# The RWKV-7 chunk scan of a hybrid encoder, rewritten from block-diagonal 128x128 matmuls to matmuls on 64x64 tiles of the array

## The chip, the cores and the metric

The kernel runs on one core of a Trainium2 chip. The metric is the device time of one execution in microseconds (us); lower is better. Engines are named as in the profile: PE is the matmul engine and PEld its weight loads, DVE the vector engine, ACT the scalar engine, POOL the GpSimd, SP the queue that issues most DMAs.

## The reference

Two layers on 256 + 1024 = 1280 tokens of width 1024 (16 heads of 64). Layer 0 mixes tokens with a bidirectional RWKV-7 recurrence, layer 1 with neighbourhood attention; a squared-ReLU MLP follows each. The change lies in the recurrence of layer 0, which is this, for each head and both directions:

```
def _wkv_scan(r, w, k, v, a, b, reverse):
    def step(S, inp):
        r_t, w_t, k_t, v_t, a_t, b_t = inp
        sa = jnp.einsum('bhvk,bhk->bhv', S, a_t)
        S = S * w_t[:, :, None, :] + sa[..., None] * b_t[:, :, None, :] + v_t[..., None] * k_t[:, :, None, :]
        return S, jnp.einsum('bhvk,bhk->bhv', S, r_t)
...
    mu = jnp.mean(y, axis=-1, keepdims=True)
    var = jnp.mean(jnp.square(y - mu), axis=-1, keepdims=True)
    y = ((y - mu) * lax.rsqrt(var + GN_EPS)).reshape(B, T, C) * lnx_g + lnx_b
    y = y + (bonus * vf).reshape(B, T, C)
    out = (y.astype(h.dtype) * g) @ w_o
```

## The kernel before

The recurrence is computed in chunks of 64 tokens. For a chunk, products of the decayed vectors a, r with b, k give 64x64 matrices; the one of a and b is unit-triangular and is inverted; then the chunk needs only matmuls with the 64x64 state S of a head.

**Jobs and units.** The work is cut into ten *jobs* (`self.jobs`, L721): two of the short sequence, eight of the long one. A job has 16 chunks of a pair of heads (two heads of 64 lie in the 128 partitions) and runs them forwards (d = 0) and backwards (d = 1). A *unit* is one step of both directions, so the scan has 160 units.

**Order.** Nothing is scheduled by the compiler: every piece is a closure with a due time in units, put on a list by `at(time, ...)`, sorted, and recorded in that order (`manual_schedule`); each engine takes its instructions in that order. Job j is due from 16 j on. Pieces whose last argument is level 1 or 2 (job 0's early work) run already during the v projection, before `scan()`.

**The chain of a unit** (`scan_step`, once for each direction, half a unit apart): `s0` multiplies k-products with v into `w` (L1012); `s1` adds ar.S (L1023) and copies the two diagonal 64x64 blocks to `up` (L1027); `s2` multiplies with the inverse (L1032), copies to `hv` (L1034) and, in `s2c`, the two blocks to `u` (L1041); `s3` makes the new state (L1046), which DVE scales block by block (L1054) and adds to the decayed old one that POOL made (`sd`, L1016); `s4` adds the rest of the output (L1060), which ACT or DVE puts into `y` (L1063, L1065). Each of these is one 128x128 matmul on a block-diagonal operand: half of each such operand is zeros.

**The work beside the chain**, done for groups of four chunks, eight groups a job, one every two units: `prod` (a.b products, L812, masked by DVE, L814), `kprod` (k products, L953, copied by ACT, masked by POOL, L958), `ktr` (transposes, L967, copied by ACT, L970), and the inverse. Its 32x32 halves are inverted on DVE for a whole job at once: 31 rank-1 steps (`rank1`), two DVE instructions each (L857, L859), laid over ten units; the halves are joined by 32x32 matmuls (`merge1` L903, `merge2` L921). Operands come by DMA, some of them twice, because the block-diagonal copies (`bb`, `bdk`, `vt`) are loaded apart.

**After the chain** `scan_post` normalises each half of a job's outputs on DVE (L1116 to L1163), ACT (square) and POOL (gain and bias), transposes it on PE (L1168) and stores it. `gate_begin` puts loads and splits for the next stage beside the last job. PSUM: three rotating buffers (`aps`) for the work beside the chain, five banks for the chain.

Of the kernel before, what the change touches and what calls it, by code (L numbers as in the profile page):

```python
# [23 lines left out]
NEG = -1e30  # L24
L2_EPS = 1e-24
# [3 lines left out]
V_QG, V_KG = 136, 137  # L29
NVEC = 138  # L30
# [18 lines left out]
class Trunk:  # L49
    def __init__(self, ctx, tc, a):  # L50
# [16 lines left out]
        self.dall = self.cp.tile([P, 8, 2, 20], F32, name="dall")  # L67
        self.bonus = self.cp.tile([P, 10, NH], F32, name="bonus")
# [33 lines left out]
    def l0_proj(self):  # L102
# [10 lines left out]
        W = 1283  # L113

# [400 lines left out]
    def prep_open(self, bctx):  # L515
        nc, tc, a = self.nc, self.tc, self.a
        self.ar_d = self.dram("ar_d", [8, 2, P, 20, P])
        self.bk_d = self.dram("bk_d", [8, 2, P, 20, P])
# [117 lines left out]
    def prep_products(self, U, h, i):  # L636
# [7 lines left out]
        if "ar" not in u:  # L644
            for nm in ("ar", "bk"):
                u[nm] = pk.tile([P, 8, P], F32, name=nm, tag=nm)
            u["kd"] = pk.tile([P, 512], F32, name="kd", tag=f"kd{d}", bufs=2)
            u["st"] = [(self.ar_d[m, d, :, ch0:ch0 + nch, :], u["ar"][:, :nch, :]), (self.bk_d[m, d, :, ch0:ch0 + nch, :], u["bk"][:, :nch, :])]
        ar, bk, kd = u["ar"], u["bk"], u["kd"][:, :w]
        if i == 0:  # L650
            nc.vector.tensor_tensor(out=ar[:, :nch, 64:128], in0=c3(r), in1=ec[:, :nch, 1 - d:65 - d], op=ALU.mult)
# [4 lines left out]
        elif i == 3:  # L656
            nc.vector.tensor_tensor(out=bk[:, :nch, 64:128], in0=c3(kd), in1=emc, op=ALU.mult)
        elif i == 4:
            nc.vector.scalar_tensor_tensor(out=tha, in0=tha, scalar=1.0, in1=kk, op0=ALU.add, op1=ALU.mult)
        elif i == 5:  # L660
            nc.vector.scalar_tensor_tensor(out=ar[:, :nch, 0:64], in0=c3(kk), scalar=-1.0, in1=ec[:, :nch, d:64 + d], op0=ALU.mult, op1=ALU.mult)
        elif i == 6:
            nc.vector.scalar_tensor_tensor(out=bk[:, :nch, 0:64], in0=c3(tha), scalar=0.5, in1=emc, op0=ALU.mult, op1=ALU.mult)
# [25 lines left out]
    def prep_bonus(self, U, h, step):  # L689
# [6 lines left out]
        elif step == 1:  # L696
            u["pb"] = self.ppn.tile([P, 8], F32, name="bps", tag="bps")
            for b in range(nb):
                nc.tensor.matmul(u["pb"][:, 2 * b:2 * b + 2], u["kd"][:, b * P:(b + 1) * P], self.blk, start=True, stop=True)
        else:  # L700
            nc.vector.tensor_copy(self.bonus[:, c0 // P:c0 // P + nb, 2 * m:2 * m + 2], u["pb"][:, :2 * nb].rearrange("p (b h) -> p b h", h=2))
# [6 lines left out]
    def scan_begin(self):  # L708
# [8 lines left out]
        self.r_hv, self.r_v2, self.r_q = ([[er.tile(shape, F32, name=name + "0")], 0] for name, shape in  # L717
                                          (("hv", [P, 16, P]), ("v2", [P, 16, P]), ("qq", [P, 16, 2, 64])))
        self.r_bb, self.r_ar, self.r_zb = ([[er.tile([P, 4, P], F32, name=f"{name}{i}") for i in range(n)], 0] for name, n in
                                           (("bb", 3), ("ar", 10), ("zb", 10)))  # L720
        for t in self.r_bb[0]:  # L721
            nc.gpsimd.memset(t, 0.0)
# [17 lines left out]
    def scan(self):  # L740
        nc, tc, pool = self.nc, self.tc, self.spool
        rp = self.rp = pool("rp", 1)
        fx = pool("fx", 1)

        def grow(r, pl, name, shape, n=1):
            r[0] += [pl.tile(shape, F32, name=f"{name}{len(r[0]) + i}") for i in range(n)]
        grow(self.r_hv, fx, "hv", [P, 16, P])
        grow(self.r_v2, fx, "v2", [P, 16, P])
        grow(self.r_q, fx, "qq", [P, 16, 2, 64])
        grow(self.r_ar, rp, "ar", [P, 4, P], 10)  # L750
        grow(self.r_zb, rp, "zb", [P, 4, P], 10)
        self.r_bk, self.r_u2, self.r_u1, self.r_s = [[], 0], [[], 0], [[], 0], [[], 0]
        grow(self.r_bk, fx, "bdk", [P, 4, P], 2)
        self.sp = pool("sp", 4)
# [3 lines left out]
        self.pbank = [self.pw.tile([P, 2, P], F32, name=f"us{d}") for d in range(2)]  # L758
        for r, nm, n in ((self.r_u2, "u2", 4), (self.r_u1, "u1", 3), (self.r_s, "S", 4)):
            grow(r, fx, nm, [P, P], n)  # L760
        for r in (self.r_bk, self.r_v2, self.r_u2, self.r_u1, self.r_s, self.r_q):
            for t in r[0]:
                nc.gpsimd.memset(t, 0.0)
# [13 lines left out]
    def scan_job(self, j):  # L777
# [4 lines left out]
        J = {"ar": {}, "zb": {}, "zk": {}, "lt": {}}  # L782
        order = [(0, 0), (1, 3), (0, 1), (1, 2), (0, 2), (1, 1), (0, 3), (1, 0)]


        T0 = -34.0

        def first(J=J):
            J["dd"] = [self.dsc.tile([16, 2, 64, 64], F32, name="dd", tag="dd") for _ in range(2)]
        at(T0, first, min(j + 1, 3))  # L790
        for n, (d, g) in enumerate(order):
            m, c0 = grp[g]
            t = T0 + 2 * n
            E = 1 if j == 0 else 2 if j == 1 and n < 2 else 3

            def load(d=d, g=g, m=m, c0=c0):
                ar = self.nxt(self.r_ar)
                nc.sync.dma_start(ar, self.ar_d[m, d, :, c0:c0 + 4, :])
                bb = self.nxt(self.r_bb)
                for e in range(2):  # L800
                    es = slice(64 * e, 64 * e + 64)
                    nc.sync.dma_start(bb[es, :, es], self.bk_d[m, d, es, c0:c0 + 4, 0:64])
                J["ar"][d, g], J["bb", d, g] = ar, bb

            def prod(c, d=d, g=g):
                ar, bb = J["ar"][d, g], J["bb", d, g]
                if c == 0:
# [1153 lines left out]
```

## Time and profile before

| what | value |
|---|---|
| median of 3 runs | 4312.45 us (4303.99 to 4316.88) |
| the profiled execution: its own time, its span | 4314.01 us, 4312.1 us |
| first and last `s0` matmul of the scan (L1012) | 763.7 and 1561.9 us |
| busy over the span | PE 3991.1, PEld 3342.6, DVE 2660.7, ACT 1813.1, POOL 1426.1 us |
| granted TensorE clock, mean | 0.958 |

The page has the span in 40 slices of 107.8 us; the scan lies in slices 8 to 15. A matmul of fp32 operands appears in the profile as two records (640 for the 320 matmuls of L1012), each with its own weight load; a record lasts from its start to the end of its pipeline, so that records in a row overlap, and the distance of their starts, not their length, is what they cost PE.

### The profile page before, as it was taken

Reading aid. Unit: us, or ns where it says so; the run is one execution under the profiler, and the core shown is the slowest. Engines: PE = TensorE matmul, PEld = TensorE weight load, DVE = VectorE, ACT = ScalarE, POOL = GpSimd, SP = SyncE. Lnnn points to the kernel's source line nnn. Section 1 sums busy time; section 2 is a strip of 40 time slices with the busy share of each in tenths; the row PEclk is TensorE's granted clock in tenths of the full one; section 3 lists DMA queues with packets and bytes.
Section 4 is the critical chain, followed back from the end, with each engine's and each line's share of the span. In section 5 each row is a group of like instructions: output and inputs, shape, how many; then the busy total and the mean of one; then the engine's idle time right before and its main releaser. Section 6 shows DMA issues by size and latency. Waiting matters only on the chain.

```text
span 4312.1 us, 69598 instructions
## 1 busy us (share of the span) xinstructions
PE 3991.1 (93%) x25060; PEld 3342.6 (78%) x25060; DVE 2660.7 (62%) x5390; ACT 1813.1 (42%) x4803; POOL 1426.1 (33%) x1498
## 2 busy tenths in 40 slices
PE   7888878888998879999999998999998999999999
PEld 4665668777777758888888888877676888888888
DVE  7889963577787654755555555166665655555555
ACT  6766641677777753111111123355554311111111
POOL 5440001234444443422222234144444432222222
PEclk9997879899999989999999999999998999999999
DMA  3335565566666434111111104333335211111111
GB/s 120 81 107 198 196 201 144 141 157 155 153 151 153 108 97 133 38 39 36 40 35 40 40 31 152 117 72 77 78 70 161 65 40 40 40 35 39 35 40 59
DMA packets 484537, 400.25 MB, mean 93 GB/s; under 512 B 289216, under 2 KB 392864, under 8 KB 484192
## 3 DMA queue, kind: packets, MB, share of 16 engines
q1 hardware_dynamic: 447968, 328.56, 28.1%
q10 hardware_dynamic: 34416, 61.35, 3.9%
q0 software_dynamic: 1808, 5.90, 0.4%
q8 instruction: 197, 3.23, 0.3%
q14 instruction: 148, 1.21, 0.1%
HBM read 285.66 MB, written 121.24 MB: 94 GB/s over the span
## 4 chain that ended last, share of the span: by engine, by line
PE 69%; DVE 14%; ACT 6%; DMA 5%; issue 4%; POOL 2%; SPq 1%; ACTq 0%; DVEq 0%; POOLq 0%
PE ps L97 17%; PE ps L99 16%; PE ps L98 16%; PE w L1060 2%; PE us L1032 2%; PE kps L953 1%; PE aps L812 1%; PE vps L503 1%; PE vps L505 1%; PE vps L504 1%; PE op L1876 1%; PE us L1046 1%; PE w L1012 1%; DVE S L1054 1%; ACT u L1041 1%
## 5 line engine op out<-in xcount | busy, mean ns | idle before, releaser
L1433 DVE TENSOR_TENSOR x<-ps,x 128x256 f32<-128x256 f32 x1488 | 814.1, 595 | 628.3 <-PE ps L99 628.0
L97 PE MATMUL ps<-ah,whi 128*128 128x512 f32 (+1 forms) x2304 | 843.1, 366 | 5.0 <-ACT whi L91 4.2
L99 PE MATMUL ps<-ah,wlo 128*128 128x512 f32 (+1 forms) x2304 | 824.0, 358 | 2.1 <-POOL wlo L92 2.0
L98 PE MATMUL ps<-al,whi 128*128 128x512 f32 (+1 forms) x2304 | 823.5, 357 | 2.6 <-POOL al L1323 2.6
L92 POOL TENSOR_TENSOR wlo<-raw,whi 128x1024 fp32r<-128x1024 f32 (+1 forms) x178 | 390.5, 2194 | 851.9 <-ACT whi L91 807.8
L97 PE MATMUL ps<-hh,whi 128*128 128x512 f32 (+1 forms) x1536 | 546.9, 356 | 13.8 <-DVE x L1433 13.8
L99 PE MATMUL ps<-hh,wlo 128*128 128x512 f32 (+1 forms) x1536 | 545.9, 355 | 0.0
L98 PE MATMUL ps<-hl,whi 128*128 128x512 f32 (+1 forms) x1536 | 545.2, 355 | 0.0
L97 PEld LDWEIGHTS ps<-ah,whi 128*128 128x128 f32 x2304 | 438.8, 190 | 80.2 <-issue 13.1
L91 ACT CAST whi<-raw 128x1024 fp32r<-128x1024 f32 (+1 forms) x206 | 200.7, 975 | 696.5 <-PE ps L98 630.6
L99 PEld LDWEIGHTS ps<-ah,wlo 128*128 128x128 f32 x2304 | 437.8, 190 | 67.8 <-POOL wlo L92 2.9
L98 PEld LDWEIGHTS ps<-al,whi 128*128 128x128 f32 x2304 | 438.5, 190 | 63.0 <-POOL al L1323 2.9
L1412 POOL TENSOR_TENSOR rl<-rl 128x512 f32<-128x512 f32 (+1 forms) x192 | 174.3, 908 | 500.6 <-PE ps L99 458.3
L97 PEld LDWEIGHTS ps<-hh,whi 128*128 128x128 f32 x1536 | 291.4, 190 | 57.4 <-DVE x L1433 16.8
L1411 ACT ACTIVATE rl<-ps 128x512 f32<-128x512 f32 (+1 forms) x192 | 100.8, 525 | 546.4 <-PE ps L99 546.4
L98 PEld LDWEIGHTS ps<-hl,whi 128*128 128x128 f32 x1536 | 291.4, 190 | 41.0
L99 PEld LDWEIGHTS ps<-hh,wlo 128*128 128x128 f32 x1536 | 291.4, 190 | 41.1
L1414 ACT CAST hh<-rl 128x512 fp32r<-128x512 f32 (+1 forms) x192 | 105.5, 549 | 321.0 <-POOL rl L1412 320.9
L1054 DVE SCALAR_TENSOR_TENSOR S<-us,dall,sd 64x64 f32<-64x64 f32 x512 | 145.0, 283 | 126.4 <-PE us L1046 115.7
L1415 DVE TENSOR_TENSOR hl<-rl,hh 128x512 fp32r<-128x512 f32 (+1 forms) x192 | 119.4, 622 | 151.6 <-ACT hh L1414 151.1
L1016 POOL TENSOR_TENSOR sd<-S,dall 128x128 f32<-128x128 f32 x256 | 122.5, 480 | 258.2 <-DVE S L1054 174.8
L1060 PE MATMUL w<-u,zb 128*128 128x128 f32 x640 | 158.2, 330 | 47.0 <-ACT u L1041 44.8
(310 smaller groups left out, 8222.4 us busy)
## 6 DMA issues: line engine op xcount, KB each, us to landing
raw<-in_w_down_dram SPq DMA_DIRECT2D x64, 512.0 KB, 3.5
raw<-in_w_up_dram SPq DMA_DIRECT2D x64, 512.0 KB, 3.4
ar<-ar_d SPq DMA_DIRECT2D x80, 256.0 KB, 3.4
bk<-bk_d SPq DMA_DIRECT2D x80, 256.0 KB, 3.5
ar_d<-ar ACTq DMA_DIRECT2D x32, 512.0 KB, 2.7
bk_d<-bk ACTq DMA_DIRECT2D x32, 512.0 KB
bs<-tab SPq DMA_DIRECT2D x128, 96.0 KB, 3.9
v_d<-vt ACTq DMA_DIRECT2D x80, 128.0 KB, 4.0
```

What stands on the lines that cost most here:

```text
L91: nc.scalar.copy(hi[:, cs], raw)
L92: lo_eng.tensor_tensor(out=lo[:, cs], in0=raw, in1=hi[:, cs].bitcast(F32), op=ALU.subtract)
L97: mm(ps, sh, mh, start=first, stop=False)
L98: mm(ps, sh, ml, start=False, stop=False)
L99: mm(ps, sl, mh, start=False, stop=last)
L1016: nc.gpsimd.tensor_tensor(out=R["sd"], in0=st["S"], in1=self.dall[:, m, d, ch:ch + 1].to_broadcast([P, P]), op=ALU.mult)
L1054: nc.vector.scalar_tensor_tensor(out=S2[es, es], in0=sn[es, es], scalar=D, in1=R["sd"][es, es], op0=ALU.mult, op1=ALU.add)
L1060: nc.tensor.matmul(w, J["zb"][d, g][:, c, :], R["u2"], start=False, stop=True, skip_group_check=True)
L1412: nc.gpsimd.tensor_tensor(out=r[:, :n], in0=r[:, :n], in1=r[:, :n], op=ALU.mult)
L1414: nc.scalar.copy(hh[:, :n], r[:, :n])
L1415: nc.vector.tensor_tensor(out=hl[:, :n], in0=r[:, :n], in1=hh[:, :n].bitcast(F32), op=ALU.subtract)
L1433: nc.vector.tensor_tensor(out=xv, in0=ps[:, :n], in1=xv, op=ALU.add)
```

## The change

- All scan matmuls become 64x64: operands of head 0 lie in partitions 0 to 63, of head 1 in 64 to 127, and `HALVES` runs over both. A matmul takes the row strip of its operands and the column strip of its output, so (0,0), (0,64), (64,0), (64,64) are four tiles. Block-diagonal copies and their DMAs go.
- One step treats both directions: `s1` adds a.S, r.S and (through the identity) S itself into three PSUM banks; ACT copies 128x128 (`s1c`, `s2c`) and writes the new state with two scaled copies (`s3c`). DVE and POOL no longer touch S.
- `kprod` masks straight from PSUM on DVE, `ktr` yields two transposes, all of them in the same three `aps` buffers. `merge1`/`merge2` become 64x64 matmuls on a zero-filled inverse, which POOL clears for each job (`qclear`).
- `rank1`: the threshold that closes a slot of half a unit goes from 877.08 to 930.0, and the start from T1 + 2.77 to T1 + 1.9.
- `scan_post`: the output stays in halves by head; gain and bias are applied after the transpose by one ACT instruction for each run; bonus times v is transposed apart; POOL has no part. `prep_bonus`, `ar_d`/`bk_d`, `dall`, `bonus` change layout; `gate_begin` changes due times.

The core of the diff (`-` before, `+` after):

```diff
-            load += 400 + 2 * jj * (32 - jj)
-            if load > 877.08:
+            if load > 930.0:
...
+            def prod(h, d=d, g=g):
+                    for c in (2 * h, 2 * h + 1):
+                        for es, eo in HALVES:
+                            mm(J["pa"][es, c], J["bb", d, g][es, c], J["aa", d, g][es, c], start=True, stop=True)
...
+                        for es, eo in HALVES:
+                            mm(J["pb"][es, c], bb[es, c], rr[es, c], start=True, stop=True)
+                            mm(J["pk"][eo, c, 0:64], kk[es, c], aa[es, c], start=True, stop=True)
+                        for es, eo in HALVES:
+                            mm(J["pk"][eo, c, 64:128], kk[es, c], rr[es, c], start=True, stop=True)
+                    nc.vector.tensor_tensor(out=zk, in0=J["pk"], in1=b4(self.mask[d], P), op=ALU.mult)
+                    nc.vector.tensor_tensor(out=zr, in0=J["pb"], in1=b4(self.mask[d][:, 64:128], 64), op=ALU.mult)
...
-            nc.tensor.matmul(R["w"], J["zk"][d, g][:, c, :], J["vt"][:, cc, :], start=True, stop=new)
+                for es, eo in HALVES:
+                    mm(A[es, d], zk[eo, c, 0:64], v[eo, cc], d == 0, new)
+                    mm(Y[eo, yd], zk[eo, c, 64:128], v[eo, cc], d == 0, False)
+                    for es, eo in HALVES:
+                        mm(sn[es, d], J["lk", d, g][eo, c], v[eo, cc], d == 0, False)
...
-                nc.tensor.matmul(w, J["ar"][d, g][:, c, :], S, start=False, stop=True)
+                for es, eo in HALVES:
+                    mm(A[es, d], J["aa", d, g][es, c], S[es, d], False, True)
+                    mm(Y[eo, yd], J["rr", d, g][es, c], S[es, d], False, False)
+                        mm(sn[es, d], self.ident[es, es], S[es, d], False, False)
+            nc.scalar.copy(R["up"], A)
...
-            nc.tensor.matmul(us, J["Q"][:, cc].rearrange("p d t -> p (d t)"), R["up"], start=True, stop=True)
+                    mm(U[es, d], J["Q"][es, cc, d], R["up"][es, d], True, True)
+            nc.scalar.copy(R["u"], U)
...
-                    nc.vector.scalar_tensor_tensor(out=S2[es, es], in0=sn[es, es], scalar=D, in1=R["sd"][es, es], op0=ALU.mult, op1=ALU.add)
+                        mm(sn[es, d], J["lb", d, g][es, c], R["u"][es, d], False, True)
+                    mm(Y[eo, yd], J["zr", d, g][es, c], R["u"][es, d], False, True)
+                nc.scalar.activation(S[:, d], sn[:, d], AF.Copy, scale=self.dall[:, m, d, ch:ch + 1])
...
+            def tr(src, nm, st=st):
+                for b in range(8):
+                    for es, eo in HALVES:
+                        nc.tensor.matmul(ps[es, b], src()[eo, b // 4, b % 4], self.ident[eo, eo], start=True, stop=True)
```

How the order of instructions moves, at three places (a row is a line of the source, the operation, out<-in, and the shape; rows of the change have the line numbers of the changed file, where L993 is the helper through which the chain's matmuls go).

PE, before, in the middle of a job: one direction's half of a unit, from its `s4` to the next one's `s4`.

```order
L1060 MATMUL w<-u_7184,zb_7159 128x128
L1012 MATMUL w<-v_6174,zk 128x128
L1032 MATMUL us_7181<-u_7188,qq_6175 128x128
L1023 MATMUL w<-S_7191,ar_7149 128x128
L812 MATMUL aps<-ar_6187,bb_6178 128x128 x2
L1046 MATMUL us_7180<-hv_6173,lt 128x128
L812 MATMUL aps<-ar_6187,bb_6178 128x128 x2
L1060 MATMUL w<-u_7185,zb_7160 128x128
```

PE, after: the end of `s1` of a unit, then `prod` of a group, `s2`, and half of the next unit's `s0` (`ba` is the bank A, `by` Y, `bs` the state's bank, `vv` is v, `cst` holds the identity).

```order
L993 MATMUL ba<-S,aa_7398 64x64
L993 MATMUL by_7443<-S,rr 64x64
L993 MATMUL bs_7445<-S,cst 64x64 x4
L812 MATMUL aps<-aa_6427,bb_6436 64x64 x8
L993 MATMUL by_7442<-up,qq_6417 64x64 x4
L993 MATMUL ba<-vv_6416,zk 64x64
L993 MATMUL by_7442<-vv_6416,zk 64x64
L993 MATMUL ba<-vv_6416,zk 64x64
L993 MATMUL by_7442<-vv_6416,zk 64x64
L993 MATMUL bs_7444<-vv_6416,lk 64x64 x2
```

Eight matmuls of 128 columns stood in half a unit; now a whole unit has 36 of 64 columns in the chain, and eight stand between `s1` and `s2` where two waits of the chain lie.

DVE, before, while a job's inverse is made: rank-1 pairs (`tmp`, `q`) between the state's updates (`S`) of the two directions.

```order
L857 TENSOR_TENSOR tmp<-mt,q 128x252
L859 TENSOR_TENSOR q<-q,tmp 128x14x18
L1054 SCALAR_TENSOR_TENSOR S_7189<-us_7181,dall,sd 64x64 x2
L857 TENSOR_TENSOR tmp<-mt,q 128x247
L859 TENSOR_TENSOR q<-q,tmp 128x13x19
L1054 SCALAR_TENSOR_TENSOR S_7190<-us_7180,dall,sd 64x64 x2
L814 TENSOR_TENSOR zb_6189<-aps,cst 128x512
```

DVE, after, in the same stretch: the pairs stand beside the masks that free PSUM (`zk`, `zr`, `za`) and the norm's first half (`bv`, `mu`).

```order
L858 TENSOR_TENSOR tmp<-mt,q 128x220
L860 TENSOR_TENSOR q<-q,tmp 128x22x10
L948 TENSOR_TENSOR zk<-kps,cst 128x512
L951 TENSOR_TENSOR zr<-bps,cst 128x256
L858 TENSOR_TENSOR tmp<-mt,q 128x231
L860 TENSOR_TENSOR q<-q,tmp 128x21x11
L858 TENSOR_TENSOR tmp<-mt,q 128x240
L860 TENSOR_TENSOR q<-q,tmp 128x20x12
L1097 TENSOR_TENSOR bv<-vv_7391,bonus 128x512
L815 TENSOR_TENSOR za_6440<-aps,cst 128x256
L1101 TENSOR_REDUCE mu<-y 128x8
L1102 TENSOR_SCALAR mu<-mu 128x8
```

The state's updates have left DVE; the masks and the norm have come closer to the rank-1 pairs, of which four now fall in each unit.

ACT, after, one unit: the chain's three copies, the state's two scaled copies among them, with a copy beside the chain (`yt`).

```order
L1034 COPY up<-ba 128x128
L908 COPY yt<-yps 128x256
L1045 COPY u<-by_7443 128x128
L1060 ACTIVATE S<-bs_7444,dall 128x64 x2
L1066 COPY y<-by_7442 128x2x64
```

Before, ACT had five copies of 64x64 or 64x128 for each direction's half unit, and the state was DVE's.

More of the change, by code (lines that the diff above doesn't have):

```diff
@@ L113, in l0_proj @@
         W = 1283
+        kp = self.sctx.enter_context(tc.tile_pool(name="kp", bufs=1))
+        self.dall = kp.tile([P, 8, 2, 20], F32, name="dall")
+        self.bonus = kp.tile([P, 12, 20], F32, name="bonus")
         mixctx = ExitStack()
@@ L816, in store @@
[L816 to L824 removed]
+                J["aa", d, g], J["bb", d, g] = self.nxt(self.r_aa), self.nxt(self.r_bb)
@@ L1066, in scan_step @@
[L1066 to L1071 removed]
+                nc.vector.tensor_tensor(out=y, in0=Y, in1=y, op=ALU.add)
+        at(i - 0.64, s0)
+        at(i, s1)
+        at(i + 0.1, s1c)
+        at(i + 0.3, s2)
+        at(i + 0.38, s2c)
+        at(i + 0.58, s3)
         if not end:
[L1073 to L1074 removed]
+            at(i + 0.66, s3c)
+        at(i + 0.75, s4)
```

495 lines of the change are left out of this document (218 added, 277 removed).

## The prediction

> **What bounds the kernel now.** First I asked where the scan stands and how busy each engine is in it. Busy time by stretches, a job in the middle, the last job, the stretch ahead of the scan (columns: length, busy time and instructions of each engine, granted clock, DMA share, GB/s):
>
> ```profile
> core 0: us, PE busy (x) PEld busy (x) DVE busy (x) ACT busy (x) POOL busy (x), PEclk, DMA share, GB/s
> 1003.00:1082.00 79.00, 70.41 (x733) 61.37 (x732) 62.34 (x168) 58.27 (x230) 37.52 (x65) 1.00 0.66 157
> 1480.00:1562.00 82.00, 66.40 (x605) 55.81 (x605) 39.32 (x113) 59.89 (x233) 36.46 (x56) 0.95 0.28 83
> 700.00:763.00 63.00, 48.80 (x379) 46.90 (x378) 24.64 (x60) 7.72 (x20) 11.95 (x25) 0.83 0.53 134
> ```
>
> A job takes some 80 us, a unit 5.0, and the last job as long, though DVE has only 39 us to do there: DVE does not set the pace now. The line of the first matmul of each step says how long the scan is:
>
> ```profile
> L1012 PE MATMUL w<-v,zk x640: 275/275/421, 763.7 to 1561.9; 128*128 128x128 f32 x160
> ```
>
> From first to last start are 798 us. Next, what PE pays. Groups of instructions in one job (x count | busy us, mean ns | idle before), and two stretches of the timeline:
>
> ```profile
> L1060 PE MATMUL w<-u,zb 128*128 128x128 f32 x64 | 15.6, 326 | 3.0 <-ACT u L1041 2.9
> L1046 PE MATMUL us<-hv,lt 128*128 128x128 f32 x60 | 12.5, 289 | 0.2 <-ACT hv L1034 0.2
> L812 PE MATMUL aps<-ar,bb 128*128 128x128 f32 x64 | 9.6, 275 | 0.0
> L1041 ACT COPY u<-us 64x64 f32<-64x64 f32 x64 | 13.2, 207 | 1.1
> L1034 ACT COPY hv<-us 64x128 f32<-64x128 f32 x32 | 8.4, 261 | 14.7 <-PE us L1032 14.1
> L970 ACT COPY lt<-lps 128x512 f32<-128x512 f32 x8 | 4.7, 588 | 0.1
> L1054 DVE SCALAR_TENSOR_TENSOR S<-us,dall,sd 64x64 f32<-64x64 f32 x56 | 15.9, 283 | 9.4 <-PE us L1046 8.4 <-issue 0.2
> L857 DVE TENSOR_TENSOR tmp<-mt,q 128x60 f32<-128x60 f32 (+14 forms) x29 | 11.7, 404 | 0.7
> L859 DVE TENSOR_TENSOR q<-q,tmp 128x60 f32<-128x60 f32 (+14 forms) x29 | 12.6, 435 | 1.0
> L814 DVE TENSOR_TENSOR zb<-aps,cst 128x512 f32<-128x512 f32 x8 | 5.5, 692 | 0.2
> L1065 DVE TENSOR_TENSOR y<-w,y 64x128 f32<-64x128 f32 x16 | 4.7, 292 | 2.7 <-PE w L1060 2.3
> L921 PE MATMUL qps<-qq,yt 32*32 32x32 f32 x128 | 3.6, 193 | 0.0
> ```
>
> ```profile
> 1004.22 1.06 PE L812 MATMUL aps<-ar,bb 128*128 128x128 f32 x8
> ```
>
> ```profile
> 1007.02 0.35 PE L921 MATMUL qps<-qq,yt 32*32 32x32 f32 x12
> ```
>
> Eight records of L812 take 1.06 us, one 0.275: starts lie (1.06 - 0.28) / 7 = **0.11 us** apart. A unit has 16 matmuls of 128 columns (ten in the chain, two each of `prod`, `kprod`, `ktr`), 32 records, 3.5 us; with the 32x32 ones (16 records at (0.35 - 0.19) / 11 = 0.015 us), 3.8 of 5.0 us. The remaining 1.2 us are waits in the chain. So **PE's order with the chain's waits in it** sets the pace.
>
> **Do tiles of the array work side by side?** On this everything hangs. Matmuls on two column strips (L1876), on two row strips (L1803), and the duration of one record:
>
> ```profile
> 2899.03 0.88 PE L1876 MATMUL op<-s,vs 128*64 128x128 f32 x12
> ```
>
> ```profile
> L1876 PE MATMUL op<-s,vs x288: 272/273/476, 2812.4 to 2991.8; 128*64 128x128 f32 x144
> ```
>
> ```profile
> 2902.45 0.45 PE L1803 MATMUL s<-ks,ql 64*128 64x384 f32 x2
> ```
>
> ```profile
> L1803 PE MATMUL s<-ks,ql x62: 379/442/444, 2800.9 to 2994.6; 64*128 64x384 f32 x50, 64*128 64x256 f32 x12
> ```
>
> ```profile
> L1845 PE MATMUL op<-s,vs x128: 222/222/369, 2805.4 to 3273.7; 128*64 128x64 f32 x128
> ```
>
> Twelve records of L1876 take 0.88 us: (0.88 - 0.27) / 11 = 0.055 apart, half of 0.11, so the two strips run at once. The two row strips of L1803 end within the length of one (0.442). L921 works on two tiles off one another's rows and columns, 32 columns, 0.015 where a quarter of 0.11 would be 0.028: again two at once. Four at once, two rows and two columns, no row shows. A record of 64 columns should cost its tile 0.055 us (half of 0.11), a matmul 0.11.
>
> [...]
>
> **PE after.** A unit has 12 matmuls in `s0`, 12 in `s1`, 4 in `s2`, 8 in `s3`; of a group, every two units, 8 + 8 + 8 + 24 + 16 (`prod`, two merges, `kprod`, `ktr`); the transposes of the norm 4: 72 in all, 144 records. With four tiles at once, the busiest tile counts: `s0` and `s1` four matmuls each (0.44 us), `s2` and `s3` two (0.22): 1.3. A group: `kprod` 0.88, `ktr`, `prod` and `merge1` 0.44 each, `merge2` 0.24, 2.4 in two units: 1.2. Transposes 0.2. Sum **2.8 us**. With only two at once 144 x 0.0275 = 4.0.
>
> **The chain after** has three turns to PE and back. Its handovers, from the chain of waits:
>
> ```profile
> 1092.07 0.21 ACT u L1041
> 1092.28 0.04 issue
> 1092.33 0.49 PE w L1060 x2
> ```
>
> A handover is some 0.05 us, and the first record after a wait is longer by 0.1 (0.49 for two where 0.11 + 0.28 would do). A turn is four records on a tile (3 x 0.055), the last one's 0.22 and that 0.1: 0.45 to 0.5. ACT: two copies of 128x128 at 0.26 (as L1034, 128 elements a partition), two scaled ones at 0.21 (as L1041). Sum 3 x 0.47 + 0.94 + 6 x 0.05 = 2.65 us. Since PE goes in order, the work beside the chain fills the waits but overshoots some: between `s1` and `s2` stands 0.44 of `s1` and 0.44 of `prod` or `kprod` against 0.8 of chain; between `s2` and `s3` 0.66 or, with `ktr`, 1.1 against 0.8; after `s3` 0.95 or 0.66 against 1.0. Together 2.74 and 3.08 in turn, and 0.2 for transposes: **3.1 us a unit where only PE, ACT and the chain count**. ACT has 2.1 us in it: 0.94, 0.13 for half of `y`, 0.8 beside the chain (`yt`, two `qq`, `lb`, `lk` in two units, 0.37 for 256 columns, between L1034 and L970), 0.2 in the norm.
>
> **DVE after.** The update of S goes (15.9 us a job), half of L1065, the mask L814. New are masks, at 692 ns for 512 columns and 0.42 for 256 (between L814 and L1065): `zk`, `zr`, `za` 1.54 a group. The rank-1 pairs stay: 11.7 + 12.6, with the two odd steps (an estimate) 25 us. But they stood in ten units and stand in 7.5 (two to every half unit), at units 14.5 to 22 counted from the job ahead, and there the norm now lies too. Its DVE work:
>
> ```profile
> L1156 DVE TENSOR_TENSOR y<-y,rqr 128x512 f32<-128x512 f32 x18 | 18.3, 1018 | 0.2
> L1120 DVE TENSOR_TENSOR y<-y,mu 128x512 f32<-128x512 f32 x18 | 14.2, 786 | 0.3
> L1163 DVE TENSOR_TENSOR y<-y,vt 128x512 f32<-128x512 f32 x18 | 13.6, 755 | 2.1 <-POOL y L1160 1.6
> L1116 DVE TENSOR_REDUCE mu<-y 128x8 f32<-128x512 f32 x18 | 12.2, 678 | 0.1
> L1128 DVE TENSOR_REDUCE va<-ysq 128x8 f32<-128x512 f32 x18 | 12.1, 673 | 0.6 <-ACT ysq L1124 0.6
> ```
>
> A half is 5.3 us (these, another 0.75 for bonus times v, 0.7 for small ones); one and a half of them, 8, fall into the stretch. So 7.5 units hold 25 + 3.75 x 1.54 + 8 + 0.6 (`y`) = 39.4 us, **5.3 a unit**, against 3.1 on PE. This cannot be hidden: three `aps` buffers go round, `prod` needs one that `zr` frees and `merge1` the one that `za` frees, and both masks stand behind rank-1 pairs on DVE. A job is then 39.4 + 8.5 x 3.1 = 66 us; the last one has no rank-1 work, 50. Nine and one: 644 us instead of 798: **-154**.
>
> **Around it.** Ahead of the scan, 700 to 763, DMA is half busy and PE waits for it; the loads are fewer, but the sequence is as long: -5 (between -15 and +10). The tail loses two gain multiplies on DVE: -6 (0 to -10). Before the scan, `prep_bonus` (24 times) and job 0's `prod` (8) are 64x64 among 128x128 matmuls. A change of tile shape costs PE an idle moment, here before L1803:
>
> ```profile
>   issue: 6.3, 25
> ```
>
> that is 0.25 us, twice for each, at most 16 us if PE sets the pace there; in the middle of that part PE is 0.85 busy and DVE 0.93, so I take half, +8:
>
> ```profile
> 400.00:500.00 100.00, 84.86 (x360) 59.98 (x359) 92.67 (x167) 65.73 (x141) 0.00 (x0) 0.86 0.53 195
> ```
>
> DMA share in the job is 0.66 of 79 us, 52; no load is added and the doubled ones (`bb`, `bdk`, `vt`) fall away, so it stays below 52 of 66: not the bound. POOL's memset of the inverse is one a job, with nothing behind it for units; the later stages do not change.
>
> Sum: -154 - 5 - 6 + 8 = -157 against the profiled execution's 4314, which lies 2 us above the median: **4157 us**.
>
> **Rivals.** (a) *DVE or the chain gives more*: without POOL's traffic the pairs take their shortest times and the fast units fill the lag; job 58, nine of them and 47: -229, about 4080. For it: PE would allow 3.1 throughout (-300, the floor, 4010); against it: the pairs' place. (b) *Two tiles at once, not four*: PE 4.0 and the chain's overshoots make 4.3 a unit; a job 39.4 + 8.5 x 4.3 = 76, the last 69: 753, -45, 4266. Hand-overs between four engines that come late by 0.5 us a unit end between this and the forecast. (c) *Slower: small records do not follow one another so closely for long.* Place: PE in all 160 units. If each record takes its 0.055 alone, a unit is 144 x 0.055 = 7.9 us, 1267 in all: 4314 + 469 = 4783. It decides from 5.0 / 144 = 0.035 us a record on. Against it: the rows above; for it: they are bursts of 12 records, after which PE waits, and in no job does PE have more than 733 in 79 us, one in 0.11. [...] (d) *No change*: DVE's stretch takes back what the fast units give, within 0.3% (about what a measurement of this kernel can tell from no change).
>
> **How the numbers follow.** Forecast (4100 to 4230): 0.54. (a) 0.10; (b) with late hand-overs 0.17; (d) 0.05; (c) 0.14. Faster by over 0.3% is the first three, 0.81; within it 0.05; slower 0.14. The range leaves out (c) and the lower half of (a), 0.19: 4070 to 4310.
>
> **What would show it.** Right: starts of 64x64 records 0.03 apart or less in `s1`; units of about 3.1 us outside the rank-1 stretch and above 5 in it, with DVE busy over 0.9 there and PE waiting for `zr` or `zk`; ACT not above 0.75. Wrong: records 0.055 or more apart with PE busy throughout (b, c); units all alike (the DVE step); a long idle of PEld with no releaser (c).

## The result and the profile after

| | before | after |
|---|---|---|
| median | 4312.86 us, 4 runs (4303.99 to 4316.88) | 4207.03 us, 4 runs (4202.25 to 4209.71) |
| ratio, 95% interval | | **0.9756** (0.9738 to 0.9774) |
| profiled execution, its span | 4314.01, 4312.1 us | 4208.19, 4206.4 us |

The change made the kernel faster by 106 us. The forecast was 157, so the kernel is 50 us slower than forecast, inside the range. From the page of the kernel after: span, busy time, and the queue that carries instructions.

```profile
span 4206.4 us, 97695 instructions
...
PE 3818.0 (91%) x40500; PEld 3213.3 (76%) x40500; DVE 2466.1 (59%) x4870; ACT 1538.6 (37%) x3671; POOL 1140.4 (27%) x998
...
q8 instruction: 318, 5.21, 0.5%
```

The same two lines of the page of before:

```profile
PE 3991.1 (93%) x25060; PEld 3342.6 (78%) x25060; DVE 2660.7 (62%) x5390; ACT 1813.1 (42%) x4803; POOL 1426.1 (33%) x1498
...
q8 instruction: 197, 3.23, 0.3%
```

All engines do less, but PE has 2 x 15,440 = 30,880 instructions more, and the queue q8 carries 121 packets and 1.98 MB more: 64 bytes for each instruction (1.98 MB / 30,880), 255 instructions for each packet (30,880 / 121). All of PE's and PEld's instructions, 81,000 after and 50,120 before, are 316 and 196 times 256, and q8 has 318 and 197 packets. So I take q8 for the supply of PE's instructions, 256 in a packet of 16 KB (5.21 MB / 318). The prediction did not look at it; it decides the rest of this text.

Where the time went. First and last matmul of `s0` in the kernel after:

```profile
L993 PE MATMUL ba<-vv,zk x1280: 212/219/367, 761.5 to 1461.8; 64*64 64x64 f32 x183
```

The scan takes 700.3 us instead of 798.2: -97.9. It begins 2.2 us earlier, and the rest behind it is 5.6 us shorter. Now one job and the last one, by engine (columns as in the prediction):

```profile
core 0: us, PE busy (x) PEld busy (x) DVE busy (x) ACT busy (x) POOL busy (x), PEclk, DMA share, GB/s
976.00:1049.00 73.00, 56.61 (x2282) 51.11 (x2284) 42.39 (x115) 31.68 (x120) 7.09 (x11) 0.98 0.48 121
1409.00:1462.00 53.00, 42.55 (x1663) 37.52 (x1657) 15.15 (x34) 29.00 (x106) 9.53 (x9) 0.97 0.25 78
```

A job takes 73 us (forecast 66), the last 53 (50). I cut a job in two, at the starts of `s2` of units 6 and 14: eight units without rank-1 steps, then eight (14, 15 and 0 to 5 of the next job) with them:

```profile
1003.70:1036.90 33.20, 25.47 (x1067) 22.84 (x1059) 9.98 (x23) 13.89 (x53) 4.88 (x10) 1.00 0.57 131
1036.90:1076.40 39.50, 30.57 (x1215) 27.74 (x1209) 32.11 (x92) 17.72 (x68) 2.31 (x3) 0.96 0.42 117
```

The half with rank-1 work takes 39.5 us, near the 39.4 that were forecast for its 7.5 units. The other half takes 33.2, 4.15 us a unit, where 3.1 was forecast, and there DVE is busy 30% of the time and ACT 42%. What PE waits for in just these eight units (us in total, times, longest):

```profile
PE aps L812 <- issue: 1.9, 2, 1.5
PE bs L993 <- issue: 1.8, 3, 0.9
PE ba L993 <- issue: 1.7, 2, 1.2
PE bs L993 <- ACT u L1045: 1.2, 4, 0.3
PE bps L942 <- issue: 0.6, 1, 0.6
PE ba L993 <- ACT S L1060: 0.4, 1, 0.4
```

6.0 of 7.6 us are "issue": PE waits for nothing that the profile shows. Over the whole scan the gaps of this kind that are longer than 0.15 us add up to 68 us (88 of them). Before, there is none: in the same view of that scan every wait has a releaser, ACT and DVE above all,

```profile
PE w L1060 <- ACT u L1041: 43.2, 114, 1.5
PE us L1032 <- DVE S L1054: 15.7, 29, 0.9
PE w L1012 <- DVE y L1065: 10.9, 15, 1.5
```

and of the 88 gaps of the kernel after, 86 end 1.2 to 1.7 us behind the end of a q8 packet, though packets come only every 4 us or so. In the eight units q8 shows

```profile
q8 instruction: 8, 0.13, 1.7%
```

eight packets in 33.2 us, one every 4.15 us, each 1.7% x 16 x 33.2 / 8 = 1.1 us long. By the program a unit has 144 records on average, 288 instructions with the weight loads. The middle units, where the norm's transposes and a part of the merges are missing, have 259 in the trace. Both are more than one packet. Packet starts in the scan of after lie at least 3.34 us apart, 3.95 in the median; before, at least 8.7.

**Theory A**: a packet of 256 instructions does not come faster than every 3.4 us, some 4 us on average, and that paces the units outside the rank-1 stretch. **Theory B**: ordinary hand-overs, PSUM buffers and PE's own time do, and the gaps are only how they show. A third, that PE takes no more than one instruction every 16 ns (4.07 us / 259) and packets only follow its pace, does not fit the trace: at the fastest, 512 instructions start within 5.6 us, 11 ns each, and such a pace would not tie the ends of the gaps to the ends of packets.

### The profile page after: what moved, and what is told of

It reads as the page before. It is cut to its first block, busy times and chain, and to the rows that moved or that the text cites. A ratio compares the mean times of both kernels' runs of the same rounds, so it can differ in the third digit from the quotient of the medians.

```text
span 4206.4 us, 97695 instructions
## 1 busy us (share of the span) xinstructions
PE 3818.0 (91%) x40500; PEld 3213.3 (76%) x40500; DVE 2466.1 (59%) x4870; ACT 1538.6 (37%) x3671; POOL 1140.4 (27%) x998
## 3 DMA queue, kind: packets, MB, share of 16 engines
q8 instruction: 318, 5.21, 0.5%
## 4 chain that ended last, share of the span: by engine, by line
PE 71%; DVE 15%; ACT 5%; issue 5%; DMA 3%; POOL 1%; SPq 1%; ACTq 0%; DVEq 0%; POOLq 0%
PE ps L96 17%; PE ps L97 17%; PE ps L98 17%; PE by L993 2%; PE bs L993 2%; PE vps L506 1%; PE vps L507 1%; PE vps L508 1%; PE ba L993 1%; PE op L1849 1%; DVE tmp L858 1%; DVE q L860 1%; PE pt L1791 1%; PE aps L812 1%; DVE cs L623 1%
## 5 line engine op out<-in xcount | busy, mean ns | idle before, releaser
L1784 POOL TENSOR_TENSOR s<-s,mx 128x384 f32<-128x384 f32 (+1 forms) x154 | 116.8, 769 | 207.4 <-DVE mx L1783 136.1
L1068 DVE TENSOR_TENSOR y<-by,y 128x128 f32<-128x128 f32 x80 | 24.6, 308 | 175.7 <-PE by L993 164.2
L1782 ACT ACTIVATE s<-s,mx 128x384 f32<-128x384 f32 (+1 forms) x154 | 87.1, 567 | 80.3 <-DVE mx L1781 78.9
```

What stands on the lines that cost most here:

```text
L1784: nc.gpsimd.tensor_tensor(out=s[:, :nk], in0=s[:, :nk], in1=mx[:, 2:3].to_broadcast([P, nk]), op=ALU.mult)
```

## The experiments

Twelve kernels, all edits of the kernel after. The table has, for each: instructions of PE in a unit by the program (mean of a job); the mean length of a unit by place, over jobs 1 to 8 (worked out from the starts of the first `by<-up,qq` record of each unit); the instructions that the trace has in a middle unit (6 to 13), and that unit's time for 256 of them; the gaps named issue over 0.15 us in the scan; the median; the ratio to before, with its interval. The differences in the text are to the runs of before taken beside each kernel (medians 4311.4 to 4314.5 us), so they can differ by some us from those of the medians.

| kernel | instr. | units 14, 15, 0-3 | 4, 5 | **6-13** | instr. in 6-13 | us per 256 there | issue us (gaps) | median | ratio (interval) |
| --- | --- | --- | --- | --- | --- | --- | --- | --- | --- |
| after | 288 | 5.38 | 3.47 | **4.07** | 259 | 4.02 | 68 (88) | 4207.0 | 0.9756 (0.9738-0.9774) |
| kk_one | 272 | 5.34 | 3.39 | **3.95** | 243 | 4.17 | 53 (73) | 4191.4 | 0.9716 (0.9703-0.9729) |
| pad8 | 320 | 5.66 | 4.07 | **4.58** | 291 | 4.03 | 66 (94) | 4285.3 | 0.9936 (0.9924-0.9949) |
| long_ktr | 288 | 5.38 | 3.55 | **4.13** | 259 | 4.07 | 52 (74) | 4209.5 | 0.9756 (0.9743-0.9769) |
| rank10 | 288 | 5.10 | 3.94 | **4.13** | 259 | 4.08 | 82 (105) | 4205.1 | 0.9748 (0.9732-0.9763) |
| pad_off | 320 | 5.71 | 3.95 | **4.72** | 291 | 4.15 | 82 (98) | 4283.2 | 0.9926 (0.9912-0.9939) |
| kb_one | 256 | 5.20 | 3.37 | **3.99** | 226 | 4.52 | 20 (36) | 4191.6 | 0.9713 (0.9699-0.9726) |
| lean | 248 | 5.29 | 3.29 | **3.84** | 219 | 4.49 | 7 (16) | 4181.2 | 0.9690 (0.9676-0.9703) |
| lean_rank10 | 248 | 5.16 | 3.32 | **4.15** | 219 | 4.85 | 14 (22) | 4195.9 | 0.9733 (0.9718-0.9748) |
| lean2 | 248 | 5.23 | 3.52 | **3.59** | 219 | 4.20 | 5 (13) | 4164.8 | 0.9660 (0.9645-0.9675) |
| lean2_rank10 | 248 | 5.08 | 3.52 | **3.61** | 219 | 4.22 | 7 (16) | 4165.4 | 0.9648 (0.9630-0.9667) |
| lean3 | 248 | 5.18 | 3.35 | **3.57** | 219 | 4.18 | 16 (36) | 4152.7 | 0.9631 (0.9611-0.9651) |
| lean3_r85 | 248 | 5.23 | 3.36 | **3.56** | 219 | 4.16 | 13 (31) | 4150.2 | 0.9628 (0.9606-0.9650) |

Over whole jobs (1 to 8), 256 instructions take 4.07 to 4.19 us in the five kernels with 288 or 320 a unit, and more in those with fewer (kk_one 4.32, lean2 4.51, lean3 4.44): with 288 or more the whole job goes at about one pace, with fewer something else counts as well.

**1. kk_one: fewer instructions, the same streaming.**

```diff
-                            mm(J["pk"][eo, c, 0:64], kk[es, c], aa[es, c], start=True, stop=True)
-                        for es, eo in HALVES:
-                            mm(J["pk"][eo, c, 64:128], kk[es, c], rr[es, c], start=True, stop=True)
+                            mm(J["pk"][eo, c].rearrange("p (h t) -> p h t", h=2), kk[es, c], J["ar", d, g][es, :, c], start=True, stop=True)
```

> aa and rr come into one tile, and kk's two multiplications by them (64 columns each) become one of 128: the same products and the same streaming time on TensorE, but 4 multiplications a unit fewer, 8 of 144 records (5.5%). Theory A, that the units without a rank-1 step wait for TensorE's instructions (packets of 256 instructions, 288 instructions a unit, 4.2 us): these 8.5 units go from 4.2 to 4.0 us, nine jobs of them make -15 to -20 us. Theory B, that these units wait for ordinary hand-overs and for TensorE's own time: no change, within 5 us.

Measured: 123 us less than before instead of 106, so 17 of the expected 15 to 20 us. The eight middle units of jobs 1 to 8 add up to 252.6 us,

```profile
sum 252.60, PE 195.04 PEld 173.36 DVE 79.30 ACT 108.31 POOL 31.86; mean PE 24.38 PEld 21.67 DVE 9.91 ACT 13.54 POOL 3.98
```

against, in the kernel after,

```profile
sum 260.30, PE 195.08 PEld 176.56 DVE 77.80 ACT 108.23 POOL 32.81; mean PE 24.39 PEld 22.07 DVE 9.73 ACT 13.53 POOL 4.10
```

PE's busy time is the same (195.04 and 195.08); only the instructions are fewer. This speaks for A, though in these units the time falls by 3.0% where the instructions fall by 6.3%; they give 7.7 of the 17 us.

**2. long_ktr: more streaming, the same instructions.**

```diff
-                            mm(J["pl"][0][es, c], J["bb", d, g][es, c], self.ident[es, es], start=True, stop=True)
+                            one = self.cst[es, es.start:es.start + P]
+                            mm(J["pl"][0][es, c], J["bb", d, g][es, c], one, start=True, stop=True)
...
```

The transposes of `kk` change in the same way.

> The transposes of bb and kk move 128 columns in place of 64 (the upper half is thrown away): the count of instructions is the same, TensorE streams 16 x 64 columns a group more, in four tiles at once about 0.45 us a group or 0.22 us a unit. Theory A (instruction supply): no change, within 8 us, since the streaming lies in time in which TensorE would wait. Theory B, that TensorE's time sets the fast units: 0.22 us x 8.5 units x 9 jobs = +17 us, and the late units of the last job longer as well.

Measured: 105 us less than before, as the kernel after (106). The sums of the middle units:

```profile
sum 264.00, PE 209.26 PEld 190.30 DVE 76.93 ACT 107.92 POOL 32.22; mean PE 26.16 PEld 23.79 DVE 9.62 ACT 13.49 POOL 4.03
```

PE is busy 14.2 us longer, the time grows by 3.7, and the gaps shrink from 68 to 52 us: PE's work filled gaps. A, and against PE's time as the bound.

**3. pad8: more instructions, one column each.**

```diff
+            for x in range(4):
+                for es, eo in HALVES:
+                    mm(self.b_y[(k + 1) % 2][es, 256 + x:257 + x], self.ident[es, es], self.one[es], True, True)
```

> Adds 8 multiplications of one column a unit, behind s2, into spare columns of a PSUM bank that nobody reads: 16 records, 32 instructions (11%) a unit more. Each streams one column, so TensorE's own work grows by about 0.1 to 0.2 us a unit at a standing in which the chain is waited for. Theory A (instruction supply): the fast units go from 4.2 to 4.65 us, +30 to +40 us over nine jobs, with the same number of idle stretches in which TensorE waits for nothing; units with rank-1 steps stay as they are. Theory B: at most the 0.1 us of each unit that lies on the chain, 0 to +15 us.

Measured: +77 us, twice what A expected. But the pads write the bank that `u` is copied from, and the copy waits for them too: unit 10 of the last job went from 3.0 to 3.7 us (granted clock 0.89) and the two behind it, at a clock of 0.5, from 3.0 to 4.6, although few instructions are issued there. Inconclusive; I had put a wait on the chain with the instructions.

**4. pad_off: the same pads, off the chain.** They stand behind `s3` and write the bank `b_y[k % 2]`, which only `s4` reads.

> The 8 multiplications of one column a unit of the run before, now behind s3 and into spare columns of the bank that s4 reads, so that the chain (u, S) does not wait for them: their TensorE time of about 0.4 us falls into the wait for S. They add 32 instructions a unit (11%), 2 packets of 256 a job. Theory A (a packet of instructions never comes faster than 3.4 us and on average every 4.0 us while TensorE asks for them): +30 to +60 us, 20 packets a job in place of 18, the middle units of a job from 4.2 to 4.6 us, while the late units of the last job, which issue fewer instructions, stay within 0.15 us of 3.0 us. Theory B (hand-overs and TensorE's time): 0 to +10 us, no more than the transposes of 128 columns took (+2 us) by much, since those too added 0.2 us of TensorE time a unit.

Measured: +75 us, above A's +30 to +60. Jobs 2 to 7 take 19 or 20 packets in place of 17 or 18; 2 x 4.0 x 9 = 72 us. The middle units:

```profile
sum 302.00, PE 232.95 PEld 217.88 DVE 77.84 ACT 109.69 POOL 28.82; mean PE 29.12 PEld 27.24 DVE 9.73 ACT 13.71 POOL 3.60
```

4.72 us a unit where I had said 4.6, and also the other units grew (5.38 to 5.71, 3.47 to 3.95): the supply holds the whole job back, not only its middle. Two of the last job's late units stayed at 3.0 us, three grew by 0.3 to 0.6, so the pads are not quite free there. The granted clock is lower with them, 0.87 to 1.00 in these eight stretches against 1.00, and a part of the 75 us may be its: the 19 of the 64 middle units with a mean clock under 1 took 5.27 us, the 45 others 4.49. But the middle half of job 8 has the full clock in both kernels. After, and here:

```profile
1366.80:1397.80 31.00, 22.72 (x1008) 20.50 (x1001) 7.99 (x19) 13.61 (x53) 1.71 (x4) 1.00 0.37 97
```

```profile
1429.00:1464.60 35.60, 26.12 (x1138) 23.64 (x1132) 8.02 (x19) 13.94 (x53) 1.38 (x3) 1.00 0.33 86
```

It takes 0.58 us a unit more, and PE is busy 73% of it in both. B (0 to +10 us) falls short. But PE's busy time in the middle units grows by 38 us where they grow by 42 (I had called the pads nearly free), so that the length alone does not tell instructions from PE's time here, as it does in kk_one and long_ktr. What does is that of the 98 gaps named issue 97 again end 1.2 to 1.7 us behind the end of a packet.

**5. rank10: the rank-1 steps over ten units.**

```diff
-            if load > 930.0:
+            if load > 877.08:
```

> Only the threshold of the rank-1 steps' load goes back from 930.0 to 877.08, so that they lie over ten units as before the change, not 7.5. Theory A (VectorE sets the units with rank-1 steps, instruction supply the others): the stretch grows from 37 us to about 41 us over ten units, six units of 4.2 us remain in place of 8.5, a job takes 66 us in place of 73, -35 to -65 us in all. If VectorE's load in these units did not matter: within 8 us.

Measured: 109 us less than before, 3 to 4 less than the kernel after, where A, with DVE's load as the bound of the first units, said -35 to -65. This part of my theory fell. The first units do get shorter (5.38 to 5.10, six of them, -1.7 us a job), but units 4 and 5 give +0.9 and the middle +0.5 back, and the gaps grow from 68 to 82 us. In the long units of the rank-1 stretch packets run ahead: in the kernel after, from the start of unit 14 to that of unit 4 (seven times, between jobs 1 and 8), q8 brings 53 packets, 13,568 instructions at 256 each, where PE and PEld start 12,473. In the two units behind, 4 and 5, it brings 14 packets, 3,584, and they start 4,321: these are short (3.47), and from there on the packet's pace holds. Who shortens the stretch only waits for instructions afterwards: 256 of them take 4.15 us in units 14 to 5 and 4.08 in the middle ones (4.26 and 4.02 in the kernel after).

**6. kb_one and lean: 32 and 40 instructions fewer.** The joined tile gets an identity behind `aa` and `rr`, so that `bb` meets `rr` and the identity in one matmul of 128 columns; lean does S times the identity in two matmuls instead of four. In these two and in lean_rank10 `lb` is copied out of its PSUM buffer after that buffer has gone to another group, so `lb` does not hold the transpose of `bb`; the instructions and columns are the same.

```diff
-                            mm(J["pb"][es, c], bb[es, c], rr[es, c], start=True, stop=True)
+                            mm(two(J["pb"][es, c]), bb[es, c], ar[es, 4 + c:9:4 - c], start=True, stop=True)
...
-                            mm(J["pl"][0][es, c], J["bb", d, g][es, c], self.ident[es, es], start=True, stop=True)
...
-                for d in range(2):
-                    for es, eo in HALVES:
-                        mm(sn[es, d], self.ident[es, es], S[es, d], False, False)
+                for es, eo in HALVES:
+                    mm(sn[es], self.ident[es, es], S[es], False, False)
```

> aa and rr stand in one tile with a 64x64 identity behind them: kk is multiplied by aa and rr at once (128 columns), bb by rr and the identity at once (128 columns), in place of four multiplications of 64 columns. 8 multiplications a unit fewer, 256 instructions a unit in place of 288 (-11%), the same columns streamed; one PSUM buffer fewer per group. The rings of tiles are a little shorter. Theory A: 16 packets a job in place of 18, -30 to -45 us against the kernel after the change. Theory B: the PSUM buffer is worth something, -10 to 0 us.

> The run before, and S times the identity in two multiplications of 128 columns a unit in place of four of 64: 248 instructions a unit (-14%), 15.5 packets a job. Theory A: -35 to -55 us against the kernel after the change, and the middle units of a job at 3.5 to 3.9 us. Theory B: -10 to +5 us.

Measured: 17 and 27 us less than the kernel after, about half of what A said, though the gaps fell to 20 and 7 us. The rest went into one unit: unit 6 took 5.5 to 8.6 us in jobs 1 to 7. In lean PE waits there for the joined tile's load,

```profile
PE ba L1000 <- DMA ar<-ar_d: 3.3, 1, 3.3
```

because my ring had 20 tiles: `s1` reads a tile until its chunks are through, and the load of the group 20 places on waits for it.

**7. lean_rank10** (the threshold 877.08 on top).

> The run before with the rank-1 steps over ten units again (threshold 877.08). With the threshold alone nothing changed (-2 us), by theory A because the instructions set the pace of the whole job on average: what the first units gained the later ones waited. With 14% fewer instructions that cover is thinner, and VectorE's load in the first units should count: another -10 to -35 us against the run before. If the rank-1 steps' load never sets the pace: within 5 us of the run before.

Measured: 15 us slower than lean. Unit 10 took 8 to 10.9 us in jobs 1 to 6: the ring's wait at another place, where PE waits 3.9 to 6.0 us for the same load. It says nothing on VectorE.

**8. lean2: the ring at 21 tiles, `lb` copied at 0.83.**

> The lean kernel (248 instructions a unit) with the ring of the joined tiles at 21 tiles again, so that a load needs not wait for a tile that the chain still reads, and lb copied out at 0.83 of its group's time, before its PSUM buffer is given on. In the lean run one unit of each of seven jobs took 6.4 to 7.3 us, waiting for that load; without it this unit should take about 3.4 us. Theory A: 7 x 3.5 = 25 us less than the lean run, about 4155 us, no unit in the middle of a job waiting for TensorE's instructions. If the stall comes from elsewhere (the end of the rank-1 steps and what follows it): as the lean run, 4175 to 4190 us.

Measured: 4164.8 us, 147 less than before and 14 less than lean, not 25. The long unit is gone (4.0 us). Middle units, 3.59 us each:

```profile
sum 229.90, PE 197.10 PEld 176.24 DVE 76.74 ACT 107.73 POOL 31.20; mean PE 24.64 PEld 22.03 DVE 9.59 ACT 13.47 POOL 3.90
```

With PE as busy as in the kernel after (197 and 195 us) these units are 30.4 us shorter, and the gaps named issue in them fall from 50 to 3 us. What PE waits for in eight of them is now the hand-overs first:

```profile
PE by L1000 <- ACT up L1040: 1.3, 4, 0.6
PE bs L1000 <- ACT u L1051: 1.1, 4, 0.3
PE ba L1000 <- ACT S L1066: 0.3, 1, 0.3
PE ba L1000 <- issue: 0.3, 2, 0.2
```

**9. lean2_rank10.**

> The run before with the rank-1 steps over ten units (877.08). In the lean run with this threshold one unit of each of six jobs took 8 to 10.9 us where 3.5 would do, some 40 us in all, waiting for a load. Theory: without it 4150 us or less, and 5 to 25 us faster than the run before it, since VectorE's units fall from 6.3 to 5.4 us while the instructions leave room. If the rank-1 steps' load does not matter even then: within 5 us of the run before it.

Measured: 4165.4 us, the same as lean2 (-146 and -147). The stretch does shrink (units 1 and 3 from 5.8 and 6.5 us to 4.9 and 5.0), but unit 14 now takes 5 to 10.6 us instead of 4.4. There, in job 0:

```profile
POOL mt L852 <- DMA mraw<-dd: 18.9, 1, 18.9
...
PE yps L914 <- DVE zk L956: 5.8, 1, 5.8
DVE q L864 <- POOL mt L852: 5.7, 1, 5.7
```

The next job's first rank-1 step stands at the head of DVE's queue and waits for its matrix, behind it `zk`, behind that PE. That the later rank-1 steps make this load late, because the matrix has one buffer, is argued and not tested. Again the gain turned into a wait.

**10. lean3 and lean3_r85: `zr` ahead of `zk`, then 8.5 units (threshold 900).**

```diff
-            for h, (dt, dl) in enumerate(((0.06, 1.4), (0.65, 1.41), (0.8, 0.83), (0.81, 1.85))):
+            for h, (dt, dl) in enumerate(((0.06, 1.4), (0.65, 1.41), (0.81, 0.83), (0.8, 1.85))):
```

> The lean2 kernel with zr ahead of zk on VectorE, so that lb, which shares zr's PSUM bank and stands ahead of the chain's up on ScalarE, waits 0.7 us less. In lean2 the units in the middle of a job alternate between 3.1 and 3.9 us, the long ones where a group's zk and zr are made. Theory: with the instructions out of the way the ordinary hand-overs set these units; four to five long ones a job fall to 3.3 to 3.5 us, 9 jobs x 4.5 x 0.4 = 10 to 20 us less than lean2. If the alternation is the instruction supply's: no change, within 5 us.

> The run before with the rank-1 steps over 8.5 units (threshold 900) in place of 7.5 or ten. Over ten units they came so late that the next job's inverse waited for its load at unit 14 (5.3 to 10.6 us in place of 4.4), which gave back what the first units gained. Theory: 8.5 units take some 2 us a job from the first units and leave the load in time: 8 to 18 us less than the run before. If the load is late again or the first units don't shrink: within 5 us.

Measured: lean3 -160 us, 13 better than lean2, with intervals that overlap. ACT's wait for `zr` in about a job (73 and 67 us) falls from

```profile
ACT lb L971 <- DVE zr L959: 6.0, 6, 1.1
```

to

```profile
ACT lb L971 <- DVE zr L959: 2.9, 8, 0.7
```

but the middle units stay (3.59 and 3.57): the gaps named issue come back, 16 us in 36 for 5 in 13, and the long units' gain (4.0 to 3.6) is lost on the short ones. So the 13 us, though inside what I had expected, did not come from the units that I had named. So at 248 instructions the supply is still close to being the bound. lean3_r85 is 2 us from lean3, no difference (expected 8 to 18): its units 14 again wait in five jobs (5.0 to 8.6 us). Both beat the kernel before and after; 4150.2 us is the best time.

## Why the prediction was right in sign and 50 us too fast

1. *PE's order with the chain's waits sets the pace before*: nothing speaks against it; before, every wait of PE in the scan has a releaser.

2. *Four tiles work side by side*: right. PE in `s1` of the kernel after, 16 records on four tiles:

```profile
1041.22 0.27 PE L993 MATMUL ba<-S,aa 64*64 64x64 f32 x1 [0.52 <-issue]
1041.22 0.27 PE L993 MATMUL by<-S,rr 64*64 64x64 f32 x1
1041.23 0.27 PE L993 MATMUL ba<-S,aa 64*64 64x64 f32 x1
1041.24 0.27 PE L993 MATMUL by<-S,rr 64*64 64x64 f32 x1
1041.32 0.22 PE L993 MATMUL ba<-S,aa 64*64 64x64 f32 x1
...
1041.38 0.22 PE L993 MATMUL ba<-S,aa 64*64 64x64 f32 x1
...
1041.44 0.22 PE L993 MATMUL ba<-S,aa 64*64 64x64 f32 x1
```

Four start within 0.02 us; the second four stand 0.10 behind the first, the later ones 0.06 apart, the 0.055 of the prediction for a record on its tile. Not every `s1` is so close: in the median the last of its 16 records starts 0.33 us after the first, here 0.24. But at the fastest 256 records in a row start within 5.6 us, 0.022 us each, and two at a time would need 0.0275. The first and third row are head 0 and head 1 in one PSUM bank, from two row strips into different partitions of it, and they start 0.01 us apart, each 0.27 long.

3. *Chain 2.65 us, units outside the rank-1 stretch 3.1*: **here the sum failed**, 8.5 x 3.1 = 26 us a job. With little work beside the chain late units of the last job take 2.96 to 3.0 us, so the chain is 0.3 longer than I had. ACT in such a unit:

```profile
1456.54 0.52 ACT L1060 ACTIVATE S<-bs,dall 128x64 f32<-128x64 f32 x2
1457.56 0.27 ACT L1034 COPY up<-ba 128x128 f32<-128x128 f32 x1 [0.50 <-PE ba L993]
...
1458.67 0.27 ACT L1045 COPY u<-by 128x128 f32<-128x128 f32 x1 [0.32 <-PE by L993]
1459.50 0.52 ACT L1060 ACTIVATE S<-bs,dall 128x64 f32<-128x64 f32 x2 [0.57 <-PE by L993]
```

From `S` to `up` are 1.02 us, to `u` 1.11, to the next `S` 0.83, where the prediction's terms make 0.99, 0.83 and 0.83: nearly all of the 0.3 lies before `u`. Its bank (`by_7442` in the order of PE shown ahead of the prediction) is the one into which the next unit's `s0` writes Y, and that `s0` stands on PE between `s2` and the copy. In five units in a row there the copy starts 0.11 us after the last of these writes ends, 0.34 after `s2`'s last record; in the scan's last unit, with no `s0` behind it, 0.05 after `s2`. So `s0`, which I had counted as work beside the chain, lies in it.

But with work beside it a middle unit takes 4.07, about one packet of instructions. That is the term that was mis-sized: PE's matmuls, ACT and the chain were counted, the supply of PE's instructions was not. Eight middle units were forecast at 24.8 us and took 32.6; the other eight at 41.0 and took 39.2. So a job came to 71.8 instead of 65.8, nine jobs 54 us, the last job 3: 57 us, all of the difference between 644 and 700.

4. *DVE: 39.4 us in 7.5 units*: the stretch has about this length (39.2 in eight), with units of over 5 us, as foretold; DVE is busy 0.81 of it (32.1 of 39.5 us), not the 0.9 that I had named as a sign. A pair is shorter than I took (20.3 us a job, not 24.3):

```profile
L860 DVE TENSOR_TENSOR q<-q,tmp 128x207 f32<-128x207 f32 (+14 forms) x29 | 10.2, 352 | 1.0
L858 DVE TENSOR_TENSOR tmp<-mt,q 128x207 f32<-128x207 f32 (+14 forms) x29 | 10.1, 348 | 0.5
```

And what I took from it, that this stretch costs the job its time, is only half true: rank10 shortens it and gains nothing, since the packets of a job come at their pace anyway. That the length came out right is in part luck: these eight units have 296 instructions each, and at the middle units' 4.02 us for 256 they would take 37 us by that alone (an estimate).

5. *Around the scan*: -5 and +8 ahead of it were forecast, -2.2 measured; -6 behind it, -5.6 measured. The 0.25 us before L1803 that the +8 starts from is, in the trace of before, idle time of PEld; PE's records start 0.27 us apart there (L1800 to L1803, 384 columns, the median), 0.18 from one L1800 to the next.

6. *Rivals.* (c), records that do not follow one another so closely for long, was the right worry with too small a chance of a mild form: a middle unit is 4.07 us for 130 records, 0.031 us each, under the 0.035 at which the sign turns. Its size (0.055 us a record) was far off: it took each record's own time, and the trace shows four starts in 0.02 us. (b), two tiles at once, gave 4.0 us for PE in a unit, close to the 4.07, but for a reason that item 2 excludes: a right number would have hidden a wrong cause. (a) had the pairs shorter, as they are, but the job did not become so; what shortened them was not tested. (d) did not occur.

What is shown: the length of a middle unit follows the count of instructions and not the columns streamed (long_ktr: 4.13 us for 4.07, with PE busy 14.2 us longer in 64 of them). With PE equally busy, 40 instructions fewer take 0.48 us off it (lean2); 32 more add 0.65 (pad_off, where PE is busier and the clock lower). Without the three kernels in which the ring made PE wait, 256 instructions take 4.0 to 4.2 us there, and the gaps end with the packets. What stays open: why a packet that takes 1.1 us comes only every 3.4 to 4 us (no run changed its path), and how much of the 3.57 us in lean3 is still supply.

## What to carry to other kernels

Before you cut matmuls into smaller tiles, count instructions per microsecond on the engine, not only columns: here four 64x64 tiles took PE's busy time in the scan from 702 to 540 us, but a unit of 288 instructions needs more than one packet of 256, and a packet came every 4 us. Idle time of PE that the view of waits calls "issue", with a packet of the instruction queue ending shortly before, was the sign of it here (86 of 88 gaps after, 97 of 98 in pad_off); a matmul of 128 columns for two of 64 with the same stationary operand gained although it streams as much (17 us in kk_one). And a load that a threshold spreads (rank10) is worth testing alone: what it freed was taken by another wait in rank10, lean2_rank10 and lean3_r85.

## What the hardware showed that I had not expected

- PE's instructions come while the program runs (170 of the 318 packets of q8 during the scan): 64 bytes each, in packets of 256 (1.98 MB and 121 packets more for 30,880 more instructions). No two packets start less than 3.2 us apart in the scan of any of these kernels; after the change the medians are 3.95 to 4.34 us. In the scan of before, of after, and of pad_off and lean2 q8 shows:

```profile
q8 instruction: 56, 0.92, 0.5%
```

```profile
q8 instruction: 170, 2.79, 1.7%
```

```profile
q8 instruction: 190, 3.11, 1.7%
```

```profile
q8 instruction: 146, 2.39, 1.6%
```

- PE has some room ahead: after units of 5 to 7 us units 4 and 5 of the kernel after run at 3.47 us (13 ns an instruction, against 16 in the middle units) before the pace of the packets holds.
- With more matmuls of one column the granted clock was lower in pad_off: 0.87 to 1.00 in its middle stretches, 1.00 in those of the kernel after, with 233 and 195 us of PE busy in 302 and 260. But pad8, with as many of them at another place, has 1.00 in six of the eight and 0.91 in two, so their number is not the reason; which it is stays open.
